# Attention of a two-layer encoder step: the query tiles of all heads as one stream, long and short in turn, decode last in each head, and later reads of y

## The chip, the cores and the metric

The program runs on one core of a Trainium2 chip. The metric is device time of one execution in microseconds (us); the number for a kernel is the median of its runs. Engines are named as in the profile: PE (TensorE; PEld is its weight load), DVE (VectorE), ACT (ScalarE), POOL (GpSimd) and SP (SyncE, which issues the DMAs).

## What is computed

Two layers, each over 1024 prompt tokens and 8 x 16 decode tokens (1152 rows, width 1024). All arithmetic is fp32; the large matrices are held as a high and a low part, so a product is three matmuls.

```
h = x @ w_in                      # pool_x, pool_gate, q, k, v, att_gate, merge_gate_a, merge_gate_b
A = (mean-pool mixer of pool_x) * silu(pool_gate)
s = q . k * 64**-0.5              # two maps (m = 0, 1) per head, 8 heads, rotary q and k
p = softmax(s);  a = p[0] - lam * p[1];  o = a @ v
B = rms_norm(o) * subln * (1 - lam_init) * silu(att_gate)
merged = sigmoid(ga) * (A @ w_a) + sigmoid(gb) * (B @ w_b)
x = layer_norm(ALPHA * x + merged @ w_o)
```

The prompt's mask lets a query see all keys up to the end of its own chunk of 64, so query tile i (128 rows, i from 0 to 7) meets 128 * (i + 1) keys: tile 7 is eight times as long as tile 0. A decode query (the item "d") sees 256 cached keys and its 16 new ones.

## The kernel before

A layer has four parts: the v columns (lines 524 to 566), q, k, the pooling and some gate columns by a product with seven multiplications (572 to 747), the rest of branch A (753 to 949), then attention with its filler (951 to 1450), and last w_b and w_o with the layer norm (1452 to 1615). The change lies in the attention part.

**Two generators are woven together there.** attention() (1280) does the heads; filler() (968) does the 16 remaining gate weights, in 384 units of three matmuls of 384 columns (line 320 to 322), with a tanh on ACT (977) after every eight units and, for the first eight weights, a product on DVE (980). attention() yields numbers; the loop at 1390 multiplies each by share (1388) and runs that many filler units, so that PE has work while softmax is under way. The numbers stand in the table STEPS (48): per item of a head a first number f1 and a second f2.

**One item of a head** goes through these pieces, each in program order on its engines:

- s1_tile (1054): scores on PE, for each m one product with the high and one with the low part of k, into ps_two, a pair of PSUM banks of which there are two. Tiles up to 3 take one pair, tiles 4 to 7 take both. soft() is its second half: DVE masks and takes the maximum (1072, or 1094 for the long ones), ACT does exp into p (1076, 1096), of which there are three buffers (one per short tile, two per long one).
- mix_tile (1101): DVE forms p[0] - c * p[1] (1105 to 1109).
- s2a_tile (1111): PE transposes the mixed p, ACT copies it out to at (1121).
- s2b_tile (1140): PE multiplies at with v, DVE copies the result (1126); do_squares then has ACT sum the squares (1130).
- "d" has the same pieces: s1_dec (1149), mix_dec, s2a_dec (1185; ten reductions on DVE, 1196 and 1198, between the transposes and the products), s2b_dec (1202).

An item's order before (1295 to 1356): s1(i); s2a of an earlier item; soft(i); squares; f1 filler; s2b of that earlier item; mix(i); f2 filler. The earlier item is two back up to n = 5, then one back; at n = 5 a second one is done, with a third number of filler. The items of a head run d, 0, 1, ... 7 (in the first head 0, 1, d, 2, 3, ... as line 1298 has it). After the last head, tile 7 is turned with a number 3 of filler and no other item beside it (1357 to 1359).

Loads for the next head are spread over the items: load_dec (1016, cached keys and new q, k, v), load_vc (1040, cached values), load_v (1010), prep_load and prep_split (881, 894: the two maps of q and k, split by two casts on ACT and two subtractions on DVE), mk_qz (1032).

**The read of y.** A head's result goes to memory (1247) and is read back (1260) when the gates of a token group are done, in the program's loop y_step (1368): it is issued, and two calls of y_step later ACT casts it into xh (1267), which waits for the transfer; DVE subtracts (1270). w_b multiplies it after that.

Of the kernel before, what the change touches and what calls it, by code (L numbers as in the profile page):

```python
# [11 lines left out]
F32 = mybir.dt.float32  # L12
# [5 lines left out]
P = 128  # L18
# [8 lines left out]
NG = 3  # L27
# [19 lines left out]
           11: (("x", 0, "t1"),), 12: (("s", 1),), 13: (("x", 1, "t2", "t3", "t4"),), 14: (("x", 1, "t1"),)}  # L47
STEPS = [(3, 2), (2, 2), (4, 1), (2, 2), (2, 2), (3, 3, 4), (3, 4), (3, 4), (4, 4)]
MG = 4
HIP = False  # L50
HEAD0 = 8
YG = 2
ENTRY_SLOTS = (1, 2, 4, 5)
# [10 lines left out]
def trunk(ctx, tc, a):  # L64
# [393 lines left out]
    for l in range(DEPTH):  # L458
# [494 lines left out]

        for tag, shape, bufs in (("osb", [P, 9, P], 2), ("gsb", [P, GW], 2), ("th", [P, GW], 3), ("atl", [P, P], 1),
                                 ("at", [P, 512], 2)):
            ap.tile(shape, F32, tag=tag, name=tag, bufs=bufs)
        for name in ("qs0", "kh0", "kl0"):
            ap.tile([P, SEQ], F32R, tag=name, name=name)
        ap.tile([P, 1024], F32, tag="p", name="p", bufs=3)
        cmask = ap.tile([P, 2, P], F32, name="cmask")  # L960
# [46 lines left out]
        groups_done = []  # L1007
        ITEMS = ["d", 0, 1, 2, 3, 4, 5, 6, 7]

# [126 lines left out]
        def do_squares():  # L1136
            while squares:
                squares.pop(0)()
# [141 lines left out]
        def attention():  # L1280
            def s2a(h, i):
                s2a_dec(h) if i == "d" else s2a_tile(h, i)
# [6 lines left out]

            load_dec(0)  # L1290
            load_v(0, 0)
            load_v(0, 1)
            prep_split(0, 1)
            yield HEAD0
            for h in range(H):
                start_head(h)
                nxt = h + 1 < H
                items = ITEMS if h else [0, 1, "d"] + ITEMS[3:]
                for n, i in enumerate(items):
                    f1, f2 = STEPS[n][:2]  # L1300
                    soft = s1_dec(h) if i == "d" else s1_tile(h, i)
                    if n == 0:
                        if h > 0:
                            s2a(h - 1, 7)
                    elif n >= 6:
                        s2a(h, items[n - 1])
                    elif n >= 2:
                        s2a(h, items[n - 2])
                    soft()
                    do_squares()  # L1310
                    yield f1
                    if n == 0:
                        if h > 0:
                            s2b(h - 1, 7)
                    elif n >= 6:
                        s2b(h, items[n - 1])
                    elif n >= 2:
                        s2b(h, items[n - 2])
                    mix(h, i)
                    if n == 5:  # L1320
                        s2a(h, items[4])
                        yield STEPS[n][2]
                        s2b(h, items[4])
                    if h == 0 and n == 0:
                        load_vc(0)
                    if h == 0 and n == 1:
                        mk_qz(0)
                    if h > 0:
                        if n == 1:
                            post_a(h - 1)  # L1330
                            g_load(h - 1, 0)
                            g_load(h - 1, 1)
                            load_v(h, 1)
                        if n == 2:
                            post_f(h - 1)
                        if 4 <= n <= 6:
                            post_b(h - 1, n - 4)
                        if n == 4:
                            g_load(h - 1, 2)
                        if n == 6:  # L1340
                            posted.append(h - 1)
                    if nxt:
                        if n == (2 if h else 3):
                            prep_load(h + 1, 0)
                        if n == 4:
                            load_dec(h + 1)
                        if n == 5:
                            prep_split(h + 1, 0)
                            prep_load(h + 1, 1)
                            load_v(h + 1, 0)  # L1350
                        if n == 7:
                            mk_qz(h + 1)
                        if n == 8:
                            prep_split(h + 1, 1)
                            load_vc(h + 1)
                    yield f2
            s2a(H - 1, 7)
            yield 3
            s2b(H - 1, 7)
            post_a(H - 1)  # L1360
# [7 lines left out]
        def y_step():  # L1368
# [7 lines left out]
            while ytodo and len(ylive) < 3:  # L1376
                (h, n), g = ytodo[0]
                if g not in groups_done or len(posted) < H - 1:
                    break
                ytodo.pop(0)  # L1380
                y_load(h, n, g)
                ylive.append([h, g, 2])

# [3 lines left out]
        W.use_f = False  # L1387
        share = len(gate_order) * NG * KD / (H * sum(map(sum, STEPS)) + HEAD0)
        due = 0.0
# [336 lines left out]
```

## Time and profile before

| what | before |
|---|---|
| median of 3 runs | 2411.27 us (2409.47 to 2414.34) |
| the profiled execution's own time | 2411.42 us |
| its span, first to last instruction | 2409.6 us |
| granted TensorE clock, mean | 0.993 |
| PE busy | 2304.1 us |
| PE weight loads busy | 2157.8 us |
| DVE busy | 1546.1 us |
| ACT busy | 977.8 us |
| attention of the first layer | from 558.7 us (first score) to about 1020 us |
| attention of the second layer | from 1752.8 us to about 2214 us |

The span lies 1.8 us under the execution's own time. In the profile L12 is line 12 of the kernel; a row of groups reads line, engine, operation, out<-in, shape, count, then busy time and the mean of one, then the engine's idle time before them and what ended it. A row of a table by stretches reads start:end, length, then for each engine its busy time with the number of its instructions, the granted clock of TensorE (1.00 is full), the DMA share and GB/s.

### The profile page before, as it was taken

To read this page: it belongs to the slowest core of one execution; us is meant where nothing else is said; L and a number is where in the kernel's file an instruction comes from. 1 tells how busy PE (TensorE), PEld (TensorE's weight loads), DVE (VectorE), ACT (ScalarE), POOL (GpSimd) and SP (SyncE) were. 2 spreads that over 40 slices of the span, in tenths; PEclk is the share of its full clock that TensorE was granted. 3 is DMA by queue.
4 is the path that set the end of the run, shared out by engine and by line. 5 is a ranking of instruction groups with operands and counts; after the bars stand their busy time and mean duration, and the time that the engine had idled before them with its cause. 6 is when DMAs were issued, how large, how long until landed. Compare 5 with 4: busy or idle time off the path is not lost.

```text
span 2409.6 us, 39819 instructions
## 1 busy us (share of the span) xinstructions
PE 2304.1 (96%) x14928; PEld 2157.8 (90%) x14928; DVE 1546.1 (64%) x2980; ACT 977.8 (41%) x2177; POOL 296.6 (12%) x312
## 2 busy tenths in 40 slices
PE   7999999998999999999999999999989999999998
PEld 6889999998888888898878999999988888889986
DVE  4477855546777777756524787546367777775855
ACT  8432234213555555523533232342145555554122
POOL 1023310000000000032100233000000000001433
PEclk9999999999999999999999999999999999999999
DMA  6643344656544554486336433445664555446942
GB/s 214 219 116 102 103 104 108 200 174 203 150 139 140 151 165 128 152 288 249 122 118 202 115 101 99 116 116 175 201 180 140 146 161 161 145 120 207 316 166 78
DMA packets 247714, 379.09 MB, mean 157 GB/s; under 512 B 49889, under 2 KB 190177, under 8 KB 247521
## 3 DMA queue, kind: packets, MB, share of 16 engines
q1 hardware_dynamic: 247520, 376.55, 50.9%
q8 instruction: 117, 1.92, 0.3%
q14 instruction: 77, 0.62, 0.1%
HBM read 259.67 MB, written 117.83 MB: 157 GB/s over the span
## 4 chain that ended last, share of the span: by engine, by line
PE 70%; DVE 11%; DMA 7%; ACT 6%; issue 4%; SPq 1%; POOL 1%; ACTq 0%; DVEq 0%; POOLq 0%
PE ps_lin L598 5%; PE ps_lin L596 5%; PE ps_lin L597 5%; PE ps_lin L320 5%; PE ps_lin L321 5%; PE ps_lin L322 5%; PE ps_tr L1144 4%; PE ps_tr L596 2%; PE ps_tr L598 2%; PE ps_tr L597 2%; PE ps_lin L335 2%; PE ps_lin L336 2%; PE ps_lin L334 2%; ACT p L1076 2%; PE ps_tr L1119 2%
## 5 line engine op out<-in xcount | busy, mean ns | idle before, releaser
L320 PE MATMUL ps_lin<-xh,wh 128*128 128x384 f32 x952 | 345.3, 363 | 1.1 <-ACT xh L1267 0.7
L322 PE MATMUL ps_lin<-xh,wl 128*128 128x384 f32 x952 | 321.3, 337 | 0.0
L321 PE MATMUL ps_lin<-xl,wh 128*128 128x384 f32 x952 | 320.7, 337 | 0.3 <-DVE xl L1270 0.2
L320 PEld LDWEIGHTS ps_lin<-xh,wh 128*128 128x128 f32 x952 | 180.4, 189 | 5.6 <-issue 2.8
L1144 PE MATMUL ps_tr<-vt,at 128*128 128x128 f32 x1152 | 156.2, 282 | 28.1 <-ACT at L1121 28.1
L1144 PEld LDWEIGHTS ps_tr<-vt,at 128*128 128x128 f32 x1152 | 147.2, 195 | 39.2 <-ACT at L1121 38.6
L321 PEld LDWEIGHTS ps_lin<-xl,wh 128*128 128x128 f32 x952 | 180.8, 190 | 1.1 <-DVE xl L1270 0.8
L322 PEld LDWEIGHTS ps_lin<-xh,wl 128*128 128x128 f32 x952 | 179.5, 189 | 0.0
L1121 ACT COPY at<-ps_tr 128x512 f32<-128x512 f32 (+1 forms) x192 | 85.8, 482 | 172.1 <-PE ps_tr L1119 172.1
L1096 ACT ACTIVATE p<-ps_two,anm 128x640 f32<-128x640 f32 (+3 forms) x128 | 122.3, 962 | 33.4 <-DVE anm L1094 29.8
L1076 ACT ACTIVATE p<-ps_two,anm 128x128 f32<-128x128 f32 (+3 forms) x128 | 66.4, 524 | 168.6 <-DVE anm L1072 160.3
L1094 DVE TENSOR_REDUCE anm<-ps_two 128x1 f32<-128x640 f32 (+3 forms) x128 | 131.2, 1025 | 4.4
L270 DVE TENSOR_TENSOR wl<-ws,wh 128x1024 fp32r<-128x1024 f32 (+1 forms) x74 | 86.0, 1162 | 70.8 <-ACT wh L265 67.6
L265 ACT CAST wh<-ws 128x1024 fp32r<-128x1024 f32 (+1 forms) x74 | 74.1, 1002 | 115.4 <-PE ps_lin L321 49.7
L640 POOL TENSOR_TENSOR tt<-tt 128x288 f32<-128x288 f32 x64 | 63.1, 986 | 420.4 <-DVE tt L639 257.2
L1108 DVE SCALAR_TENSOR_TENSOR p<-p,acc 128x128 f32<-128x128 f32 (+7 forms) x128 | 104.8, 818 | 4.5
L1086 PE MATMUL ps_two<-kh,qs 128*128 128x320 f32 (+3 forms) x256 | 91.0, 357 | 11.3 <-ACT p L1076 11.3
L1119 PE MATMUL ps_tr<-ident,p 128*128 128x128 f32 x576 | 84.4, 273 | 5.6 <-DVE r L1109 5.6
L1087 PE MATMUL ps_two<-kl,qs 128*128 128x320 f32 (+3 forms) x256 | 89.5, 352 | 0.0
L1126 DVE COPY osb<-ps_tr 128x128 f32<-128x128 f32 x144 | 41.3, 287 | 66.1 <-PE ps_tr L1144 60.4
L659 ACT COPY sb<-ps_lin 128x288 f32<-128x288 f32 x80 | 32.0, 400 | 123.3 <-PE ps_lin L598 118.8
L1119 PEld LDWEIGHTS ps_tr<-ident,p 128*128 128x128 f32 x576 | 69.2, 141 | 13.0 <-ACT xh L1267 6.2
(522 smaller groups left out, 6886.9 us busy)
## 6 DMA issues: line engine op xcount, KB each, us to landing
ws<-wt SPq DMA_DIRECT2D x96, 512.0 KB, 4.0
mt_d<-th SPq DMA_DIRECT2D x96, 192.0 KB, 3.2
fx<-q_d SPq DMA_DIRECT2D x128, 128.0 KB, 3.4
fx<-o_k SPq DMA_DIRECT2D x128, 128.0 KB, 3.3
st<-ck SPq DMA_DIRECT2D x32, 512.0 KB, 5.9
fx<-cv SPq DMA_DIRECT2D x32, 512.0 KB, 4.0
mt<-mt_d SPq DMA_DIRECT2D x42, 384.0 KB, 5.8
xT_d<-xs SPq DMA_DIRECT2D x36, 256.0 KB, 2.6
```

Source lines behind the costliest of these rows:

```text
L320: PE.matmul(ps, wh[:, k, :], xh[:, k, :], start=(k == 0), stop=False),
L321: PE.matmul(ps, wh[:, k, :], xl[:, k, :], start=False, stop=False),
L322: PE.matmul(ps, wl[:, k, :], xh[:, k, :], start=False, stop=(k == nk - 1)))
L596: PE.matmul(ps, wh[:, k, :], oh[:, k, :], start=first and k == 0, stop=False, **more)
L597: PE.matmul(ps, wh[:, k, :], ol[:, k, :], start=False, stop=False, **more)
L598: PE.matmul(ps, wl[:, k, :], oh[:, k, :], start=False, stop=k == 3, **more)
L1076: S.activation(out=pt[m], in_=s[:, m, :n], func=AF.Exp, bias=nm[:, m:m + 1], accum_out=ls_[:, m:m + 1])
L1094: V.tensor_reduce(out=nm[:, m:m + 1], in_=s[:, :, :c], axis=AX.XY, op=ALU.max, negate=True)
L1096: S.activation(out=p[:, :n].rearrange("p (b c) -> p b c", b=2), in_=s[:, :, :c], func=AF.Exp, bias=nm[:, m:m + 1], accum_out=ls_[:, m:m + 1])
L1108: V.scalar_tensor_tensor(out=pt[0], in0=pt[1], scalar=cc, in1=pt[0], op0=ALU.mult, op1=ALU.add)
L1119: PE.transpose(tr[:, j * P:(j + 1) * P], p[:, (b0 + j) * P:(b0 + j + 1) * P], ident)
L1144: PE.matmul(o_ps, hd["at", i][b // 4][:, (b % 4) * P:(b % 4 + 1) * P], hd["vt", b // 4][:, b % 4, :], start=(b == 0), stop=(b == i))
```

## The change

The heads become one list, flow, of (head, position n, item) triples, with the items of a head in the order 7, 3, 6, 2, 5, 1, 4, 0, d (in the last head 7, 3, 6, 2, 5, d, 4, 1, 0). At each step j the program does s1 of item j, s2a of item j - 2, soft of item j, mix of item j - 1, squares, f1 filler, s2b of item j - 2, f2 filler. So every item is turned two steps after its scores, across the border of heads too, and its mix is one step later than before and stands behind the next item's maximum on DVE. The doubled step n = 5 and its third number go.

share leaves REST = 28 units of the filler out of attention; what is left runs after it. STEPS sums to 52 per head instead of 54.

The loads move: load_dec and load_vc are of the same head now (n = 2 and n = 8; in the last head load_vc at n = 3), mk_qz at n = 6 (last head: 4), load_v's second half at n = 0, prep_split of map 1 before the scores of n = 8; post_a, post_f and post_b at n = 2, 3 and 5 to 7.

A read of y is cast five calls of y_step after its issue instead of two. Last, the list that reserved tiles at the head of the attention pool goes, so its tiles lie at other addresses.

```
-STEPS = [(3, 2), (2, 2), (4, 1), (2, 2), (2, 2), (3, 3, 4), (3, 4), (3, 4), (4, 4)]
+STEPS = [(2, 3), (5, 1), (3, 2), (3, 4), (3, 2), (3, 4), (3, 2), (3, 3), (3, 3)]
+REST = 28
...
-        ITEMS = ["d", 0, 1, 2, 3, 4, 5, 6, 7]
+        ITEMS = [7, 3, 6, 2, 5, 1, 4, 0, "d"]
+        LAST = [7, 3, 6, 2, 5, "d", 4, 1, 0]
...
+            flow = [(h, n, i) for h in range(H) for n, i in enumerate(ITEMS if h < H - 1 else LAST)]
+            for j in range(len(flow) + 2):
+                h, n, i = flow[j] if j < len(flow) else (H, j - len(flow), None)
+                back = flow[j - 2] if j >= 2 else None
...
+                if n == 8 and not last:
+                    if h + 1 < H:
+                        prep_split(h + 1, 1)
+                soft = None
+                if i is not None:
                     soft = s1_dec(h) if i == "d" else s1_tile(h, i)
...
+                if back:
+                    s2a(back[0], back[2])
+                if soft:
                     soft()
+                if 0 < j <= len(flow):
+                    mix(flow[j - 1][0], flow[j - 1][2])
+                do_squares()
+                yield f1
+                if back:
+                    s2b(back[0], back[2])
...
-                ylive.append([h, g, 2])
+                ylive.append([h, g, 5])
...
-        share = len(gate_order) * NG * KD / (H * sum(map(sum, STEPS)) + HEAD0)
+        share = (len(gate_order) * NG * KD - REST) / (H * sum(map(sum, STEPS)) + HEAD0)
```

Each engine has as many instructions of each kind as before; only their places differ. Three places follow.

**ACT, fourth head of the first layer.** Before, the stretch in the middle of the head, from the copy of tile 2's transposes (at, 384 columns) to the casts for the next head. L1096 is exp, L1130 a square, L977 the filler's tanh, L265 the split of a filler weight, L902 and L903 the casts of the next head's q and k.

```order
L1121 COPY at<-ps_tr 128x384
L1096 ACTIVATE p,als<-ps_two,anm 128x640 x2
L1130 ACTIVATE jk,ss<-osb 128x128
L977 ACTIVATE th<-ps_lin 128x384
L265 CAST wh<-ws 128x1024
L1121 COPY at<-ps_tr 128x512
L902 CAST qs<-fx 128x1024
L903 CAST kh<-fx 128x1024
```

After, the same head from tile 7's copies on: L1117 is the copy, L1092 and L1072 exp, L972 the tanh.

```order
L1117 COPY at<-ps_tr 128x512 x2
L1092 ACTIVATE p,als<-ps_two,anm 128x896 x2
L1126 ACTIVATE jk,ss<-osb 128x128 x2
L1117 COPY at<-ps_tr 128x512
L1072 ACTIVATE p,als<-ps_two,anm 128x384 x2
L972 ACTIVATE th<-ps_lin 128x384
L1117 COPY at<-ps_tr 128x512
L1117 COPY at<-ps_tr 128x384
L1092 ACTIVATE p,als<-ps_two,anm 128x768 x2
```

Before, the copy of tile 3 (512 columns) stands behind tile 4's exp of the same step, a square, a tanh and a cast. After, each step's copies stand ahead of that step's exp and behind the exp of the step before.

**DVE, the decode item at the start of the fifth head of the first layer.** Before: mix of tile 0 (L1108), the previous head's post_a (L1224 to L1226), the ten reductions of the decode item (L1196, L1198), then the maximum of tile 1.

```order
L1108 SCALAR_TENSOR_TENSOR p<-p,acc 128x128
L1109 RECIPROCAL r_8287<-als 128x1
L1224 TENSOR_TENSOR wv__8383<-r_7629 128x9
L1225 TENSOR_TENSOR wv__8383<-wv__8383,ss 128x9
L1226 TENSOR_SCALAR wv__8383<-wv__8383 128x9
L1196 TENSOR_REDUCE azt<-ps_tr 128x2x16 x4
L1198 TENSOR_REDUCE atl<-ps_tr 128x64
L1196 TENSOR_REDUCE azt<-ps_tr 128x2x16 x4
L1198 TENSOR_REDUCE atl<-ps_tr 128x64
L1071 MEMSET ps_two 64x2x64
L1072 TENSOR_REDUCE anm<-ps_two 128x2
```

After: the same ten reductions (L1192, L1194, of the fourth head's decode item) stand at n = 1 of the fifth head.

```order
L1192 TENSOR_REDUCE azt<-ps_tr 128x2x16 x4
L1194 TENSOR_REDUCE atl<-ps_tr 128x64
L1192 TENSOR_REDUCE azt<-ps_tr 128x2x16 x4
L1194 TENSOR_REDUCE atl<-ps_tr 128x64
L1067 MEMSET ps_two 64x2x64
L1068 TENSOR_REDUCE anm<-ps_two 128x2
L1101 RECIPROCAL ar_8259<-als 128x1
L1103 SCALAR_TENSOR_TENSOR acc<-als,nlam,ar_8259 128x1
L1104 SCALAR_TENSOR_TENSOR p<-p,acc 128x1024
L1105 RECIPROCAL r_8174<-als 128x1
L1122 COPY osb<-ps_tr 128x128
```

They stand ahead of tile 3's maximum (L1068) and of tile 7's mix (L1104, 1024 columns), which the next step's transposes read.

**ACT, end of the first layer's attention.** Before, with the casts of y (L1267) and the last two tiles:

```order
L1267 CAST xh<-fx 128x2x384
L1121 COPY at<-ps_tr 128x512
L1121 COPY at<-ps_tr 128x384
L1096 ACTIVATE p,als<-ps_two,anm 128x1024 x2
L1130 ACTIVATE jk,ss<-osb 128x128
L1267 CAST xh<-fx 128x384
L1267 CAST xh<-fx 128x2x384 x3
L1121 COPY at<-ps_tr 128x512 x2
L977 ACTIVATE th<-ps_lin 128x384
```

After, with L1263 for the casts of y, and tile 0 as the last:

```order
L1072 ACTIVATE p,als<-ps_two,anm 128x128 x2
L1126 ACTIVATE jk,ss<-osb 128x128
L972 ACTIVATE th<-ps_lin 128x384
L1117 COPY at<-ps_tr 128x256
L1126 ACTIVATE jk,ss<-osb 128x128
L972 ACTIVATE th<-ps_lin 128x384
L1263 CAST xh<-fx 128x2x384 x2
L1117 COPY at<-ps_tr 128x128
L1126 ACTIVATE jk,ss<-osb 128x128
L1263 CAST xh<-fx 128x2x384
```

Before, four casts of y stand between tile 7's exp and the copies of tile 7, the last of the attention; after, two stand between tile 0's exp and its one copy.

More of the change, by code (lines that the diff above doesn't have):

```diff
@@ L952, in trunk @@
         ap = ap_ctx.enter_context(tc.tile_pool(name=f"a2_{l}", bufs=1, reuse_waits="tile"))
[L954 to L959, printed above, removed]
         cmask = ap.tile([P, 2, P], F32, name="cmask")
@@ L1288, in mix @@
                 mix_dec(h) if i == "d" else mix_tile(h, i)
-            load_dec(0)
             load_v(0, 0)
@@ L1294, in attention @@
             yield HEAD0
[L1295 to L1300, printed above, removed]
-                    soft = s1_dec(h) if i == "d" else s1_tile(h, i)
[L1302 to L1308, printed above, removed]
-                    soft()
[L1310 to L1319, printed above, removed]
-                    if n == 5:
[L1321 to L1343, printed above, removed]
-                            prep_load(h + 1, 0)
[L1345 to L1356, printed above, removed]
@@ L1357, in attention @@
-            s2a(H - 1, 7)
-            yield 3
-            s2b(H - 1, 7)
+            flow = [(h, n, i) for h in range(H) for n, i in enumerate(ITEMS if h < H - 1 else LAST)]
+            for j in range(len(flow) + 2):
+                h, n, i = flow[j] if j < len(flow) else (H, j - len(flow), None)
+                back = flow[j - 2] if j >= 2 else None
+                last = h == H - 1
+                f1, f2 = STEPS[n]
+                if n == 0 and h < H:
+                    start_head(h)
+                if n == 8 and not last:
[3 more added lines that the diff above has]
+                if i is not None:
+                    soft = s1_dec(h) if i == "d" else s1_tile(h, i)
+                if back:
+                    s2a(back[0], back[2])
+                if soft:
+                    soft()
+                if 0 < j <= len(flow):
[4 more added lines that the diff above has]
+                    s2b(back[0], back[2])
+                if h > 0 and n == 0 and h < H:
+                    load_v(h, 1)
+                if 0 < h < H:
+                    if n == 2:
+                        post_a(h - 1)
+                        g_load(h - 1, 0)
+                        g_load(h - 1, 1)
+                    if n == 3:
+                        post_f(h - 1)
+                    if 5 <= n <= 7:
+                        post_b(h - 1, n - 5)
+                    if n == 5:
+                        g_load(h - 1, 2)
+                    if n == 7:
+                        posted.append(h - 1)
+                if h < H:
+                    if n == 2:
+                        load_dec(h)
+                        if h + 1 < H:
+                            prep_load(h + 1, 0)
+                    if n == 3 and last:
+                        load_vc(h)
+                    if n == (4 if last else 6):
+                        mk_qz(h)
+                if h + 1 < H:
+                    if n == 5:
+                        prep_split(h + 1, 0)
+                        prep_load(h + 1, 1)
+                        load_v(h + 1, 0)
+                    if n == 8:
+                        load_vc(h)
+                yield f2
```

## The prediction

> **What bounds the kernel now.** I read the page first, then a table by stretches (one stretch per head of the attention), then PE's waits inside the attention, then the timeline of one wait.
>
> ```profile
> PE 2304.1 (96%) x14928; PEld 2157.8 (90%) x14928; DVE 1546.1 (64%) x2980; ACT 977.8 (41%) x2177; POOL 296.6 (12%) x312
> ```
>
> PE is the bound: 2304.1 of 2409.6 us busy, so 105.5 us idle in all. The change has as many instructions of each kind as before, hence PE's own work stays and only its idle time and its clock can move. The heads of the first layer, with PE, PEld, DVE, ACT and POOL busy in each stretch and then the clock:
>
> ```profile
> 558.00:604.00 46.00, 40.00 (x275) 36.41 (x274) 32.07 (x80) 19.98 (x56) 0.00 (x0) 0.96 0.67 196
> ...
> 660.00:715.00 55.00, 51.21 (x371) 47.46 (x370) 42.11 (x102) 28.70 (x77) 2.11 (x3) 1.00 0.48 142
> ...
> 934.00:989.00 55.00, 53.90 (x392) 50.30 (x391) 38.13 (x98) 29.10 (x81) 2.00 (x2) 1.00 0.28 89
> 989.00:1020.00 31.00, 27.30 (x155) 25.65 (x153) 20.52 (x35) 17.09 (x32) 2.00 (x2) 0.89 0.57 177
> sum 462.00, PE 431.45 PEld 400.64 DVE 339.31 ACT 244.45 POOL 16.62; mean PE 47.94 PEld 44.52 DVE 37.70 ACT 27.16 POOL 1.85
> ```
>
> And the second layer's attention in the same cut:
>
> ```profile
> 1752.00:1798.00 46.00, 38.83 (x267) 35.14 (x266) 30.59 (x78) 18.78 (x53) 0.00 (x0) 0.96 0.65 195
> ...
> 2183.00:2214.00 31.00, 27.33 (x162) 25.27 (x160) 21.84 (x36) 17.34 (x32) 2.00 (x2) 0.94 0.59 181
> sum 462.00, PE 430.46 PEld 399.17 DVE 339.47 ACT 244.34 POOL 16.62; mean PE 47.83 PEld 44.35 DVE 37.72 ACT 27.15 POOL 1.85
> ```
>
> PE is idle 462 - 431.45 = 30.6 us in one layer's attention and 462 - 430.46 = 31.5 us in the other: 62.1 of the 105.5 us. It is worst at the start (6.0 us of 46), about 3.8 us in the third head (55 - 51.21), 1.1 us near the end of the heads, and 3.7 us again after them. Its clock falls below full in the first and the last stretch. What ended PE's waits in the first layer's attention:
>
> ```profile
> PE ps_tr L1144 <- ACT at L1121: 14.3, 14, 1.9
> PE ps_two L1086 <- ACT p L1076: 5.7, 7, 1.0
> ...
> PE ps_two L1157 <- DMA vt<-o_v: 2.6, 1, 2.6
> ```
>
> Twenty of the 30.6 us are ACT's: the copy of transposes before the product with v, and exp, which frees the scores' PSUM; a load ends just one wait, of 2.6 us. One wait for a copy on ACT's timeline, in the fourth head:
>
> ```profile
> 755.71 0.80 ACT L1096 ACTIVATE p<-ps_two,anm 128x640 f32<-128x640 f32 x1
> ...
> 756.78 0.48 ACT L977 ACTIVATE th<-ps_lin 128x384 f32<-128x384 f32 x1
> 757.16 1.04 ACT L265 CAST wh<-ws 128x1024 fp32r<-128x1024 f32 x1
> 758.09 0.59 ACT L1121 COPY at<-ps_tr 128x512 f32<-128x512 f32 x1
> ```
>
> The copy is the last of a queue: exp, tanh and cast go first, and PE's product with v comes only after it. ACT is busy for 28.7 of the 55 us of the head before, so this is its order and not its load.
>
> **The change part by part.** *The stream.* With the copies ahead of their step's exp, a copy waits only for what ACT has left over from the step before. Such a step lasts about 5.5 us: a head's busy PE time is 51.2 us and loses 3.4 of its 47.1 filler units (54 x 0.873 before, 52 x 0.840 after). A unit by PE's timeline:
>
> ```profile
> 992.24 0.35 PE L320 MATMUL ps_lin<-xh,wh 128*128 128x384 f32 x1
> ...
> 992.78 0.33 PE L320 MATMUL ps_lin<-xh,wh 128*128 128x384 f32 x1
> ```
>
> One unit is 0.54 us from start to start, so a head has 51.2 - 3.4 x 0.54 = 49.4 us of PE work in nine steps. ACT has 28.7 us per head, 3.2 per step, and between transposes and product stand some 2.5 units, 1.35 us, against a copy of 0.59. I take both ACT waits as gone in most steps. Long and short items in turn also mean that tiles 4 to 7, which take both PSUM pairs, never follow one another.
>
> *What is late next is DVE.* It has 42.1 us per head; in heads of 49.4 us that is 85%, where it was 77%. Its durations in the fourth head:
>
> ```profile
> L980 DVE SCALAR_TENSOR_TENSOR th<-th,ps_lin 128x384 f32<-128x384 f32 x5 | 2.8, 550 | 3.6 <-ACT th L977 3.6
> L1108 DVE SCALAR_TENSOR_TENSOR p<-p,acc 128x1024 f32<-128x1024 f32 x2 | 2.6, 1284 | 0.1
> L1126 DVE COPY osb<-ps_tr 128x128 f32<-128x128 f32 x9 | 2.6, 284 | 1.9 <-PE ps_tr L1144 1.4 <-PE ps_tr L1214 0.5
> ...
> L1094 DVE TENSOR_REDUCE anm<-ps_two 128x1 f32<-128x1024 f32 x2 | 2.4, 1224 | 0.1
> L270 DVE TENSOR_TENSOR wl<-ws,wh 128x1024 fp32r<-128x1024 f32 x2 | 2.4, 1214 | 0.0
> ...
> L1072 DVE TENSOR_REDUCE anm<-ps_two 128x2 f32<-128x1024 f32 x1 | 1.2, 1224 | 0.0
> L1196 DVE TENSOR_REDUCE azt<-ps_tr 128x32 f32<-128x64 f32 x8 | 1.2, 216 | 0.0
> ...
> L1198 DVE TENSOR_REDUCE atl<-ps_tr 128x64 f32<-128x128 f32 x2 | 0.6, 282 | 0.0
> ```
>
> The narrowest place is n = 1, where the decode item's ten reductions stand ahead of tile 3's maximum and tile 7's mix. From tile 7's scores to its mix DVE has two maxima (2.45), a copy (0.28), ten reductions (8 x 0.216 + 2 x 0.282 = 2.29), tile 3's maximum (1.22) and the mix (1.28): 7.5 us, and 9.5 us with the masks, reciprocals and the decode item's scaling, which I put at 2. If a filler weight falls there, L980 and L270 add 1.76: 11.3 us. PE takes two steps, 11 us, to the transposes that read the mix. So it fits, or is late by up to 1 us when a weight falls there; L270 also waits for ACT's cast. Ends: nothing per head, or today's 3.8 us. I take 1.2 us, nearer the sum than today's row, which is another queue's.
>
> *The ends.* The first score now starts with tile 7 instead of tile 0, and the decode item of the first head, third before, comes ninth. The last item is tile 0 instead of 7. The rows, with PE busy and then the clock:
>
> ```profile
> 558.90:561.40 2.50, 1.00 (x6) 1.00 0.79 224
> 565.80:568.70 2.90, 0.41 (x3) 1.00 0.90 211
> 570.00:574.50 4.50, 4.50 (x24) 0.62 0.53 190
> 996.00:999.40 3.40, 0.62 (x4) 1.00 0.77 211
> 1001.00:1002.50 1.50, 0.82 (x4) 0.50 0.49 127
> ```
>
> The 1.5 us at 558.9 (the split of the second map is late) stays by 0.8, since the four longer products of the first map cover the rest. The 2.5 us before the decode item (its values were still loading) and the 2.8 us before tile 7's transposes go. In the last head the decode reductions, 2.29 us, have three yields, 2.5 units or 1.35 us, of cover: 0.9 us is lost there, new. The later cast of y means that ACT no longer waits for a transfer ahead of an exp or a copy; y's chain then has the filler that runs after the attention as cover (28 units less 9 in the stream's two last steps, 19 x 0.54 = 10.3 us), without which it would cost up to the 3.7 us of today's last stretch. I keep 0.5 us for it. The loads that move on SP (load_dec beside prep_load at n = 2, load_vc) are issued five or more us ahead of their use, and no wait of the heads after the first is for a load today: nothing, or at worst one wait of 2.5 us per layer like that of the first head. The reserved tiles change addresses and first waits only: nothing, within the same bound.
>
> *The clock.* The row at 0.62 follows the 2.5 us wait, the one at 0.50 the 2.8 us wait. Over the stretches the loss is 46 x 0.04 + 31 x 0.11 in the first layer and 46 x 0.04 + 31 x 0.06 in the second: 9.0 us. It goes with those waits. The Trainium skill, page "TensorE: Matmul & The Clock Gate", section "What's actually happening", has half rate come after an idle window of about 3.4 us. Here 2.5 us were enough, so the measurement decides.
>
> *The sum.* Lost now: 62.1 idle and 9.0 clock, 71.1 us. Kept: per layer 8 x 1.2 + 0.8 + 0.9 + 0.5 = 11.8, for two 23.6 us. Gain 47.5 us. The profiled execution took 2411.4 us, 0.1 us from the median; 2411.4 - 47.5 = 2364 us.
>
> **The rivals.** *DVE takes over in part.* Each of the first five heads of a layer, where L980 runs, keeps 3.8 us: 5 x 3.8 + 3 x 1.2 + 2.2 = 24.8 per layer, gain 71.1 - 49.6 = 21.5, time 2390 us. For it: 85% of a strictly ordered queue, with each mix behind the next item's maximum, which itself waits for PE. Against: today the five slower heads have the decode item's wait as well, and DVE idles 13 us per head.
>
> *It slows down: one long wait per head at n = 1 or n = 2.* If reductions, cast, split, maximum and mix line up so that the transposes of tile 7 come late by 2.8 us in every head, the clock halves each time, which cost 4.5 x 0.38 = 1.7 us after the first decode wait. That is 4.5 us, plus 1.2 elsewhere, in 16 heads: 91 us, plus 4.4 at the ends, against 71.1 saved: 2436 us. It decides from a wait of about 2.5 us on; shorter ones only eat the gain. For it: DVE's sum of 9.5 to 11.3 us against 11. Against: it must be late in all heads, and the second half of a layer has no L980. By the Trainium skill's 3.4 us (the same page and section) a 2.8 us wait would leave the clock alone, and the time would be 2409 us; the rows of this case speak for the halving.
>
> *No change in effect.* The waits move and cost what they did, within 4.8 us. Little speaks for it: ACT's order is changed for certain, and a DVE that had just this much too little time would be chance.
>
> *More than forecast.* 0.3 us kept per head: 2 x (2.4 + 2.2) = 9.2, time 2350 us; and each wait that goes also saves a short restart of PE that its idle time doesn't show, so down to 2342.
>
> **How the numbers follow.** Forecast with its better end (2342 to 2380) 64%, DVE in part (2380 to 2402) 24%, no change 4%, slower 8%. The range from 2342 to 2396 leaves out the slower case, no change, and the ends. A measurement tells about 0.2% (4.8 us) from no change: faster 0.88, same 0.04, slower 0.08.
>
> **What would show it.** Right: PE's waits for at and p nearly absent from the attention, PE idle there below 15 us per layer, DVE at 80% or more of it, full clock in the first and last stretch, the waits left on DVE's mix or the decode reductions. Wrong: a wait of PE of over 2 us that repeats in every head, a clock below 0.95 in stretches in the middle, or ACT waiting for y's transfer ahead of a copy.

## The result

The changed kernel takes 2348.6 us (median of four runs, 2347.1 to 2351.2) against 2410.8 us for the kernel before in the same session. The ratio is 0.974, 95% interval 0.972 to 0.976: faster by 62 us, where 47.5 were forecast. Its profiled execution took 2349.3 us with a span of 2347.5 us, against 2409.6 us, so the spans differ by 62.1 us and the two traces can be laid side by side.

### The profile page after: what moved, and what is told of

Its sections match the earlier page's. It is cut to its first block, busy times and chain, and to the rows that moved or that the text cites. A ratio compares the mean times of both kernels' runs of the same rounds, so it can differ in the third digit from the quotient of the medians.

```text
span 2347.5 us, 39899 instructions
## 1 busy us (share of the span) xinstructions
PE 2288.2 (97%) x14928; PEld 2150.2 (92%) x14928; DVE 1538.9 (66%) x2980; ACT 981.8 (42%) x2177; POOL 301.8 (13%) x312
## 4 chain that ended last, share of the span: by engine, by line
PE 82%; DVE 6%; DMA 5%; ACT 3%; issue 3%; SPq 1%; POOL 1%; DVEq 0%; ACTq 0%; POOLq 0%
PE ps_lin L321 7%; PE ps_lin L322 6%; PE ps_lin L323 6%; PE ps_tr L1140 5%; PE ps_lin L597 5%; PE ps_lin L599 5%; PE ps_lin L598 5%; PE ps_tr L1115 3%; PE ps_tr L597 3%; PE ps_tr L599 2%; PE ps_tr L598 2%; PE ps_lin L336 2%; PE ps_lin L337 2%; PE ps_lin L335 2%; PE ps_two L1082 2%
## 5 line engine op out<-in xcount | busy, mean ns | idle before, releaser
L1117 ACT COPY at<-ps_tr 128x512 f32<-128x512 f32 (+2 forms) x192 | 86.8, 482 | 191.8 <-PE ps_tr L1115 191.6
L1140 PE MATMUL ps_tr<-vt,at 128*128 128x128 f32 x1152 | 150.0, 275 | 0.0
L1090 DVE TENSOR_REDUCE anm<-ps_two 128x1 f32<-128x1024 f32 (+3 forms) x128 | 131.1, 1024 | 4.4
L1092 ACT ACTIVATE p<-ps_two,anm 128x1024 f32<-128x1024 f32 (+3 forms) x128 | 122.3, 963 | 25.4 <-DVE anm L1090 22.3
L1104 DVE SCALAR_TENSOR_TENSOR p<-p,acc 128x1024 f32<-128x1024 f32 (+7 forms) x128 | 104.8, 819 | 4.5
L1072 ACT ACTIVATE p<-ps_two,anm 128x512 f32<-128x512 f32 (+3 forms) x128 | 66.5, 524 | 79.5 <-DVE ar L1101 59.9
L1115 PE MATMUL ps_tr<-ident,p 128*128 128x128 f32 x576 | 85.6, 273 | 6.4 <-ACT at L1117 4.1
L1082 PE MATMUL ps_two<-kh,qs 128*128 128x512 f32 (+3 forms) x256 | 90.0, 355 | 1.5 <-ACT p L1072 1.2
L1083 PE MATMUL ps_two<-kl,qs 128*128 128x512 f32 (+3 forms) x256 | 89.1, 351 | 0.7 <-DVE kl L906 0.7
L1115 PEld LDWEIGHTS ps_tr<-ident,p 128*128 128x128 f32 x576 | 68.7, 141 | 12.1 <-ACT at L1117 5.5
L1508 POOL TENSOR_TENSOR mg<-mt 128x384 f32<-128x384 f32 x42 | 60.0, 1433 | 115.2 <-DVE mt L1507 115.2
```

The lines of the kernel that those rows point to most:

```text
L1082: PE.matmul(s[:, b, :c], qs[:, ql], kh[:, kc], start=True, stop=False)
L1090: V.tensor_reduce(out=nm[:, m:m + 1], in_=s[:, :, :c], axis=AX.XY, op=ALU.max, negate=True)
L1092: S.activation(out=p[:, :n].rearrange("p (b c) -> p b c", b=2), in_=s[:, :, :c], func=AF.Exp, bias=nm[:, m:m + 1], accum_out=ls_[:, m:m + 1])
L1104: V.scalar_tensor_tensor(out=pt[0], in0=pt[1], scalar=cc, in1=pt[0], op0=ALU.mult, op1=ALU.add)
L1115: PE.transpose(tr[:, j * P:(j + 1) * P], p[:, (b0 + j) * P:(b0 + j + 1) * P], ident)
L1140: PE.matmul(o_ps, hd["at", i][b // 4][:, (b % 4) * P:(b % 4 + 1) * P], hd["vt", b // 4][:, b % 4, :], start=(b == 0), stop=(b == i))
```

## The profile after

The first part of the page, the engines' busy time in the changed kernel:

```profile
PE 2288.2 (97%) x14928; PEld 2150.2 (92%) x14928; DVE 1538.9 (66%) x2980; ACT 981.8 (42%) x2177; POOL 301.8 (13%) x312
```

PE has the same 14928 instructions and is busy 15.9 us less; its idle time falls from 105.5 to 59.3 us. To see where, the run is cut at the same events in both kernels: from the first score of a layer's attention to the last transposes of its results, and from there to the end of the product that follows. In each row the columns are the stretch and its length, PE, PEld, DVE, ACT and POOL busy, the clock, the DMA share and GB/s. The kernel before:

```profile
558.90:1018.20 459.30, 428.95 (x3045) 398.53 (x3045) 337.53 (x802) 243.18 (x634) 16.62 (x22) 0.99 0.50 150
1018.20:1108.20 90.00, 89.65 (x517) 89.07 (x516) 57.07 (x65) 24.60 (x30) 29.02 (x22) 1.00 0.86 298
1753.00:2211.40 458.40, 427.46 (x3045) 396.96 (x3044) 336.77 (x801) 242.74 (x634) 16.62 (x22) 0.99 0.50 150
2211.40:2301.80 90.40, 89.80 (x517) 89.01 (x516) 63.74 (x69) 12.58 (x14) 34.03 (x23) 1.00 0.89 313
```

The changed kernel, in the same four stretches:

```profile
560.20:984.80 424.60, 418.78 (x3047) 393.55 (x3045) 331.98 (x799) 243.43 (x632) 20.29 (x25) 1.00 0.54 161
984.80:1078.50 93.70, 91.17 (x516) 88.91 (x514) 58.62 (x68) 26.12 (x33) 29.26 (x22) 1.00 0.86 290
1720.60:2146.10 425.50, 418.83 (x3045) 393.37 (x3044) 333.27 (x799) 243.66 (x632) 20.29 (x25) 1.00 0.54 161
2146.10:2239.70 93.60, 92.22 (x517) 90.60 (x516) 64.20 (x71) 13.99 (x16) 33.37 (x23) 0.98 0.86 305
```

The two attentions together are 67.6 us shorter. Of that 48.8 us are idle time of PE (30.35 + 30.94 before, 5.82 + 6.67 now), and 18.8 us are busy time of PE for the same number of matmuls. The stretch behind each attention is longer by 3.7 and 3.2 us, 6.9 us given back. All the other stages make 1.4 us.

PE's waits in the first layer of the changed kernel, from just ahead of the first score on; the second layer's are the same but for the start, where PE waits 0.26 and 0.69 us for the split of the first head's maps:

```profile
PE ps_tr L1115 <- ACT at L1117: 2.0, 3, 0.7
PE ps_tr L1188 <- DVE osb L1122: 1.5, 2, 0.7
PE ps_tr L1115 <- DVE osb L1122: 1.2, 2, 0.7
PE ps_lin L321 <- DVE th L941: 1.1, 1, 1.1
PE ps_two L1082 <- ACT p L1072: 0.6, 1, 0.6
```

The 14 waits of PE's product for ACT's copy are gone; the three waits for a copy that are left are waits of transposes (L1115). In place of the seven waits for exp there are one of 0.6 us and another of 0.2. No wait in the attention is for the mix (L1104), for the decode reductions or for a load. The wait of 1.1 us lies just ahead of the first score; the longest behind it is 0.7 us, and the clock is 1.00 in both attentions.

## The experiments

The theory to start from was the prediction's: the copies stand ahead of their step's exp, the alternation keeps tiles 4 to 7 from following one another, the filler held back covers y's chain, and DVE at n = 1 is what comes next. A part that does nothing is the rival in each case. Every run was timed beside the kernel before, which took 2411.3 to 2412.0 us in these sessions.

**The distance between a read of y and its cast.**

```diff
-                ylive.append([h, g, 5])
+                ylive.append([h, g, 2])
```

> The changed kernel with y's cast two passes behind its read, as before the change, instead of five. Theory (the later reads and casts of y give part of the gain back): behind the attention the last cast of a read comes at 982.79 us and holds the direct casts of the last head back, so that PE waits 1.5 us there and runs nine products in 4.9 us instead of 1.6, 3.3 us per layer. With two passes the last read and its cast come several us earlier, these waits go and the time falls to about 2342 us. Rival (the twelve reads take 29 us whatever the distance, 951.4 to 980.3 in the changed kernel and 982.7 to 1011.4 in the one before): nothing is won behind the attention, and ACT waits for the transfer ahead of a copy again, which cost PE one wait of 3.1 us in a layer of the kernel before: 2349 to 2355 us.

> The changed kernel with y's cast three passes behind its read instead of five. Theory (late casts cost 3.3 us per layer behind the attention): between the result for two passes and 2348.6 us, nearest to two, about 2343 us. Rival (the pace of the reads is set elsewhere): 2348 to 2351 us.

Measured: 2349.8 us with two passes and 2347.7 with three, ratios 0.974 (0.973 to 0.976) and 0.973 (0.972 to 0.975). Neither differs from the changed kernel, so the rival holds: the later reads of y are worth nothing by themselves. The reads' first and last start, in the changed kernel and then with two passes:

```profile
L1256 SPq DMA_DIRECT2D fx<-y_d x12: 319/370/440, 951.4 to 980.3; - x12
```

```profile
L1256 SPq DMA_DIRECT2D fx<-y_d x12: 319/379/460, 950.6 to 978.9; - x12
```

Twelve reads take 28.9 and 28.3 us. The code says why: a group of y may be read only when the filler has done with that group's columns, and the third group's filler is the last of all. In the changed kernel its four reads start at 973.1 us and later, and PE leaves the filler at 972.4.

**No filler held back.**

```diff
-REST = 28
+REST = 0
```

> The changed kernel with no filler held back for the time behind the attention (28 units of 0.54 us are shared out among the steps as before). My prediction's term says that this filler covers y's chain: without it PE waits behind the attention by up to 15 us less what the chain now leaves, and the more filler in the heads can only win the 5 to 6 us per layer that PE still waits there; by it the time is 2358 us or more, up to 2375. Rival (y's passes are counted in filler units, so the chain shrinks with the filler, and the stream gains cover): 2345 to 2350 us.

Measured: 2365.3 us, 16.7 us more, so the prediction's term holds in sign, and its size lies near the middle of the expected range. PE's waits of this run in the last stretch of the first layer (955 to 995 us):

```profile
PE ps_tr L1140 <- ACT at L1117: 3.4, 2, 1.8
PE ps_two L322 <- DVE xl L1266: 1.7, 3, 1.0
```

The last tiles' copies come late, and the products wait for y's casts. So the 3.4 us for the copies are not those of y's chain behind the attention: on ACT one of the two copies stands behind the cast of a weight (1.04 us) and the other behind three casts of y (2.30 us).

**The same filler held back in the kernel before.**

```diff
-        share = len(gate_order) * NG * KD / (H * sum(map(sum, STEPS)) + HEAD0)
+        share = (len(gate_order) * NG * KD - 28) / (H * sum(map(sum, STEPS)) + HEAD0)
```

> The kernel before with one thing changed: 28 units of filler are held back for the time behind its attention, as in the changed kernel. Theory (the filler held back covers y's chain, and the run without it cost the changed kernel 8.3 us per layer): the last stretch of the attention, which loses 3.7 us to waits and about as much to the clock, gets most of that back, and the heads, which lose half a unit per step, give some of it up: 2398 to 2408 us. Rival (the heads of the kernel before need their filler as cover for the waits for copies and exps): 2411 to 2430 us.

Measured: 2421.1 us, ratio 1.0039 (1.0026 to 1.0052), slower by 9.4. The rival holds. So the 28 units are a gain only in the new stream. The stretch behind the attention shows something else in this run:

```profile
1021.10:1114.20 93.10, 91.89 (x517) 90.42 (x516) 58.25 (x66) 25.13 (x31) 28.85 (x21) 0.98 0.85 289
2219.10:2312.30 93.20, 91.98 (x516) 90.30 (x515) 62.66 (x71) 13.04 (x15) 32.44 (x23) 0.98 0.88 306
```

It is 3 us longer than in the kernel before, as it is in the changed kernel, and PE waits there for the same casts (0.46 and 0.45 us in each layer). With the filler held back, the 3 us lost there appear in the old order too.

**The reserved tiles.** The list that the change removed is put back.

```diff
+        for tag, shape, bufs in (("osb", [P, 9, P], 2), ("gsb", [P, GW], 2), ("th", [P, GW], 3), ("atl", [P, P], 1),
+                                 ("at", [P, 512], 2)):
+            ap.tile(shape, F32, tag=tag, name=tag, bufs=bufs)
...
         cmask = ap.tile([P, 2, P], F32, name="cmask")
```

> The changed kernel with the list of reserved tiles of the kernel before put back (osb, gsb, th, atl, at, the first head's maps and p are allocated ahead of the masks). Theory (it moves addresses and first waits only, which I put at nothing): 2348.6 us within 2. Rival (the reserved order makes the first head wait for buffers of the stage before, a wait of 2.5 us per layer as the bound had it): 2351 to 2354 us.

Measured: 2351.1 us, ratio 0.975 (0.973 to 0.976) against 0.974 (0.972 to 0.976): no difference that can be told. The median lies at the edge of the rival's range, but PE's waits in the first attention are those of the changed kernel, with none of 2.5 us. They cost nothing that these runs can tell, as forecast.

**One step behind instead of two.**

```diff
-                back = flow[j - 2] if j >= 2 else None
+                back = flow[j - 1] if j >= 1 else None
...
-                if 0 < j <= len(flow):
-                    mix(flow[j - 1][0], flow[j - 1][2])
                 do_squares()
                 yield f1
                 if back:
                     s2b(back[0], back[2])
+                if i is not None:
+                    mix(h, i)
```

> The changed kernel with every tile turned one step behind its scores instead of two; the mix then stands in the tile's own step, behind the product of the tile before. Order of the items, fillers and y stay. Theory (the second step is what takes the chain from the scores to the turning off PE's path): for a long tile two maxima (2.45 us), the second exp (0.8), and the mix (1.28) make 4.5 us ahead of the transposes, a step lasts 5.5 us of which the scores themselves take about 1, so PE waits 0.5 to 1.5 us in each of the 64 long steps, 32 to 96 us, and the time is 2380 to 2440 us. Rival (the alternation and the filler at the end carry the gain): 2348 to 2355 us.

Measured: 2501.6 us, 153 us more than the changed kernel and 90 more than the one before. The theory holds in sign, and its size was too small: the time lies 62 us beyond the range. PE's waits in the first layer:

```profile
PE ps_tr L1115 <- DVE r L1105: 25.1, 16, 2.3
PE ps_tr L1115 <- DVE p L1104: 16.4, 8, 2.9
```

Twenty-four transposes wait for the mix, or for the small operation that stands right behind it. The edit changes two things, since the mix then stands ahead of the next maxima again. The run that follows has that order of mix and maxima with the lag of two; against its 2418.1 us the second step of lag alone is worth 83 us.

**The mix ahead of the next maxima, and then ascending tiles.** The lag of two steps and the copies ahead of the exps stay in both.

```diff
+                if 0 < j <= len(flow):
+                    mix(flow[j - 1][0], flow[j - 1][2])
                 if soft:
                     soft()
-                if 0 < j <= len(flow):
-                    mix(flow[j - 1][0], flow[j - 1][2])
```

> The changed kernel with the mix of the tile before put ahead of the maxima of the next tile instead of behind them (the transposes' copies stay ahead of the exps). It is the control for the run with the tiles in ascending order, which needs this for its buffers. Theory (DVE has room, since PE's waits left in the changed kernel are 0.4 us per head and none is for the mix): 2346 to 2353 us. Rival (DVE is near its limit, and the maxima that come 1.28 us later hold the PSUM pairs and so the next scores): at least 0.5 us in each of 64 long steps, 2380 us or more.

Measured: 2418.1 us, ratio 1.003 (1.002 to 1.004). The theory was wrong and the rival holds: this one swap on DVE undoes the whole gain. PE's waits in the first layer of this run:

```profile
PE ps_two L1082 <- ACT p L1072: 12.5, 9, 2.3
PE ps_two L1063 <- ACT p L1092: 9.1, 8, 2.4
```

The waits are for exp, which has to free the PSUM pair that the next scores need. DVE in the fourth head, where tile 7's mix (L1104) now goes ahead of tile 3's maximum (L1068):

```profile
731.15 1.28 DVE L1104 SCALAR_TENSOR_TENSOR p<-p,acc 128x1024 f32<-128x1024 f32 x1
...
732.72 1.22 DVE L1068 TENSOR_REDUCE anm<-ps_two 128x2 f32<-128x1024 f32 x1
```

and ACT, idle for 4.73 us until that maximum is there, and PE's scores of tile 6 behind it:

```profile
734.04 0.69 ACT L1072 ACTIVATE p<-ps_two,anm 128x512 f32<-128x512 f32 x1 [4.73 <-DVE anm L1068]
```

```profile
735.54 0.47 PE L1082 MATMUL ps_two<-kh,qs 128*128 128x448 f32 x1 [1.13 <-ACT p L1072]
```

The mix is needed only a step later, the maximum at once. The kernel before had this order as well, since each mix stood in its own tile's step. On its DVE, ahead of the copy that the prediction showed, tile 4's maximum stands behind tile 3's mix and a product of the head before (L1243, 0.60 us), though the scores of tile 4's first map had been there since 751.1:

```profile
752.38 0.75 DVE L1108 SCALAR_TENSOR_TENSOR p<-p,acc 128x512 f32<-128x512 f32 x1
...
753.87 0.82 DVE L1094 TENSOR_REDUCE anm<-ps_two 128x1 f32<-128x640 f32 x1
```

ACT's exp of tile 4, which heads the queue in front of that copy, waits for this maximum:

```profile
754.73 0.80 ACT L1096 ACTIVATE p<-ps_two,anm 128x640 f32<-128x640 f32 x1 [1.08 <-DVE anm L1094]
```

Then, with the mix first, the tiles in ascending order:

```diff
-        ITEMS = [7, 3, 6, 2, 5, 1, 4, 0, "d"]
-        LAST = [7, 3, 6, 2, 5, "d", 4, 1, 0]
+        ITEMS = [0, 1, 2, 3, 4, 5, 6, 7, "d"]
+        LAST = [0, 1, 2, 3, 4, "d", 5, 6, 7]
```

> The changed kernel with the mix first, and the tiles of a head in ascending order, 0 to 7 and then the decode item (in the last head the decode item sixth), so that the long tiles 4 to 7 follow one another; the lag of two steps, fillers and y stay. Theory (long and short in turn matter because tiles 4 to 7 take both PSUM pairs): the waits for exp of the kernel before come back, 5.7 us per layer there, so 11 us more than the run with the mix first alone, some more with DVE's load bunched in four steps: about 2360 to 2375 us. Rival (the lag of two steps is all that counts): within 3 us of the run with the mix first.

Measured: 2434.5 us, 16.4 more than with the mix first alone, against 11 and some more expected. Its largest wait in the first layer:

```profile
PE ps_two L1082 <- ACT p L1092: 18.0, 11, 3.3
```

Long scores wait for the exp of the long tile before them. With the mix first, the alternation is worth 16 us. With the mix behind the maxima the ascending order wasn't tried, because two long tiles in a row then need four buffers for p, and the kernel has three.

**The alternation alone, in the kernel before.**

```diff
-        ITEMS = ["d", 0, 1, 2, 3, 4, 5, 6, 7]
+        ITEMS = ["d", 0, 4, 1, 5, 2, 6, 3, 7]
...
-                items = ITEMS if h else [0, 1, "d"] + ITEMS[3:]
+                items = ITEMS if h else [0, 4, "d", 1] + ITEMS[4:]
```

> The kernel before with one thing changed: the items of a head in the order d, 0, 4, 1, 5, 2, 6, 3, 7 (in the first head of a layer 0, 4, d, 1, 5, 2, 6, 3, 7); its lags (two steps, and one from the seventh item on), fillers and y stay. Theory (order alone isn't the gain, the lag of one step behind the last items stays): the waits for the copy stay at about 14 us per layer and those for exp go, 2395 to 2410 us. Rival (the order of the tiles is most of the gain): 2360 to 2375 us.

Measured: 2443.9 us, slower than the kernel before by 32.5, outside what either side expected, and the waits went the other way than the theory had it: those for the copy fall from 14.3 to 2.7 us in the first layer, and those for exp grow to

```profile
PE ps_two L1086 <- ACT p L1076: 20.8, 10, 3.4
```

from 5.7 us. The transposes (L1119) also wait 11.6 us for DVE there (2.8 us in the kernel before). So the order of the tiles alone, with the mix ahead of the maxima and a lag that changes in the middle of a head, is a loss; which of the two makes it one was not tried.

**How much room DVE has at n = 1.** Tile 3's maximum is taken once and twice more.

```diff
                     V.tensor_reduce(out=nm, in_=s[:, :, :n], axis=AX.X, op=ALU.max, negate=True)
+                    if i == 3:
+                        for _ in range(1):
+                            V.tensor_reduce(out=nm, in_=s[:, :, :n], axis=AX.X, op=ALU.max, negate=True)
```

> The changed kernel with the maximum of tile 3 taken twice (1.22 us more on DVE in each head, at the place where my sum put 9.5 to 11.3 us of DVE's work against 11 us of time). Theory (the mix of tile 7 is in time with little to spare: by the trace it ends 0.9 to 1.6 us ahead of PE's first transpose that reads it, least in the first, third and fifth head): late by 0.3 us in three or four heads per layer, 2349 to 2352 us. Rival (DVE has room, its order was the only trouble): 2348.6 us, and so still with the maximum taken three times. Second rival (DVE is late already, as my sum had it): 1.2 us in each of 16 heads, 2368 us.

> The changed kernel with the maximum of tile 3 taken three times (2.45 us more on DVE in each head). Theory (0.9 to 1.6 us to spare ahead of the transposes of tile 7): 2.45 less the spare time of each head makes 10.0 us per layer, 20 us in all, some more with the clock where a wait comes to 2.5 us: 2365 to 2375 us. Rival (DVE has room): within 3 us of 2348.6. Second rival (DVE is late already): 2.45 us in 16 heads, 2388 us or more.

Measured: 2368.8 and 2398.4 us, 20 and 50 more. Both lie beyond my theory's ranges and where "late already" had them (2368 us, and 2388 or more); the room ahead of the transposes, on which my theory rested, isn't what counts. Both runs' waits for exp in the first layer's attention (L1085 and L1075 here are L1082 and L1072 of the changed kernel):

```profile
PE ps_two L1085 <- ACT p L1075: 6.6, 8, 1.8
```

```profile
PE ps_two L1085 <- ACT p L1075: 16.7, 8, 3.1
```

One wait in every head, and in the third head it is this one:

```profile
670.77 0.47 PE L1085 MATMUL ps_two<-kh,qs 128*128 128x448 f32 x1 [1.10 <-ACT p L1075]
```

Tile 6's second map waits for tile 3's exp. The same place in the changed kernel, DVE's maximum and mix first:

```profile
665.38 1.22 DVE L1068 TENSOR_REDUCE anm<-ps_two 128x2 f32<-128x1024 f32 x1
...
666.96 1.28 DVE L1104 SCALAR_TENSOR_TENSOR p<-p,acc 128x1024 f32<-128x1024 f32 x1
```

and then ACT and PE:

```profile
667.37 0.68 ACT L1072 ACTIVATE p<-ps_two,anm 128x512 f32<-128x512 f32 x1
...
668.20 0.47 PE L1082 MATMUL ps_two<-kh,qs 128*128 128x448 f32 x1
```

The exp ends at 668.05, and the score starts 0.15 us behind it. In the runs with more DVE work every such wait ends 0.14 us behind the exp, so that is the least that these runs show, and the third head has nothing to spare. By the same reading the eight heads of a layer have 0 to 0.9 us to spare, and the first of them waits for 0.61 us in the changed kernel. Adding 1.22 us to these eight gives the eight waits of the run to within 0.15 us each. That the first run meets the 2368 us of "late already" is luck: that side had 1.2 us of wait in every head, while the waits added are 6.0 us per layer, 12.0 in all, and the rest of the 20 us is mostly PE's busy time in the two attentions (843.0 us against 837.6).

**The last head's casts ahead of y's last ones.**

```diff
         part_step(0)
+        post_b(H - 1, 0, direct=True)
+        g_load(H - 1, 2)
         part_step(1)
+        post_b(H - 1, 1, direct=True)
...
-        for g in range(NG - 1):
-            post_b(H - 1, g, direct=True)
-            if g == 0:
-                g_load(H - 1, 2)
```

> The changed kernel with the last head's own results for the first two groups turned, split and cast between the first two parts of the product with w_o, ahead of the last casts of y's reads, instead of behind them. Theory (the four reads of the third group can start only when the filler is at its end, at 973.1 us in the changed kernel, so that their last cast comes 11 us later, and the three casts of the last head queue behind it, 1.67 us each): two of the three leave that queue, and of the 3.3 us per layer 1.7 to 3.3 are won, 2342 to 2345 us. Rival (the last read alone sets the end): 2347 to 2350 us; and if the casts of the last head hold ACT or DVE up ahead of the filler's last tanh or the casts of weights, up to 2353 us.

Measured: 2352.3 us, ratio 0.9755 (0.9742 to 0.9768): nothing won, as in the second rival. ACT of this run near the end of the first attention:

```profile
976.04 0.51 ACT L1263 CAST xh<-ysb 128x384 fp32r<-128x384 f32 x1 [1.26 <-DVE ysb L1239]
980.04 0.51 ACT L1263 CAST xh<-ysb 128x384 fp32r<-128x384 f32 x1 [3.48 <-DVE ysb L1239]
980.45 2.29 ACT L1263 CAST xh<-fx 128x768 fp32r<-128x768 f32 x3
```

ACT waits 3.48 us for the last head's second group, and the three casts of y's reads stand behind it; PE then waits 2.0 us for one of them, earlier than before. The queue was only turned round.

## Why the prediction was right, and where it was not

The sign and the range were right, and so was the bound: the time was in PE's idle time and clock inside the attention. The sum came out 14.6 us short. Its terms, and what the two traces measure:

| term, both layers | forecast, us | measured, us |
|---|---|---|
| idle time of PE in the attention | -38.5 | -48.8 |
| clock and busy time of PE there | -9.0 | -18.8 |
| behind the attention | 0 | +6.9 |
| other stages | 0 | -1.4 |
| sum | -47.5 | -62.1 |

*The stream.* "With the copies ahead of their step's exp, a copy waits only for what ACT has left over" is right as far as it goes. The 14 waits of the product for the copy are gone, and they stay away in the run with the mix first (two, 0.8 us in all), which has the same lag and the same order of copies and exps. But that run loses the whole gain, to waits for exp: 21.6 us in the first layer by the two rows shown, against 5.7 in the kernel before. These exps wait for DVE, for maxima that stand behind a mix. So the place of the mix behind the next maxima is what the gain hangs on, and the prediction named it only in a rival, as a reason why DVE would be late. In the row at 755.71 I saw a full queue on ACT, read it as ACT's order, and didn't look at what had made the exp late, the 1.08 us at 754.73. The second step of lag is needed as well (83 us without it), because only with it can the mix stand behind the next maxima.

*DVE at n = 1.* The place was right and the waiter wrong. I asked whether tile 7's mix reaches the transposes in time. It does in all 16 heads, by 0.9 to 1.6 us, so the 1.2 us per head that I kept is zero: the term was too large by about 19 us. The chain that is tight there is tile 3's maximum, its exp, and tile 6's scores, with 0 to 0.9 us to spare, and it costs 0.6 us per layer. Waits that my sum did not have took part of the place: 4.7 us per layer for DVE's copies of results and for the copy of transposes.

*The ends.* The split of the first head's maps was put at 0.8 us; it costs 0.95 in the second layer (0.26 and 0.69) and, within the stretch, nothing in the first. The last head's decode item was put at 0.9 us; between its transposes (945.92) and its products (948.26) PE has no wait, so this term is zero. (The wait of 0.73 us at 911.16 in the last head is for the copy of a result, ahead of the transposes of the seventh head's decode item.) For y's chain I kept 0.5 us per layer, counted in the table's first row. This is the term that failed: the chain holds the end back behind the attention. In the second layer of the changed kernel the nine products that close the first three parts take 4.7 us there instead of 1.6, and in the first layer 4.4. Two of their rows, the first of the second and of the third three:

```profile
2148.05 0.44 PE L321 MATMUL ps_two<-xh,wh 128*128 128x384 f32 x1 [0.46 <-ACT xh L1263]
...
2149.71 0.44 PE L321 MATMUL ps_lin<-xh,wh 128*128 128x384 f32 x1 [0.45 <-ACT xh L1263]
```

Three products take 1.66 us, where 0.52 us is their pace without waits. In the second layer the clock then falls to half for some 3 us, which the stretch's 0.98 shows; in the first layer two waits of 0.60 and 0.56 us for a later product on DVE (L1507) come on top, which are not y's. The cover of 10.3 us of filler that I named ends just where the third group's reads may begin, so it cannot cover them. That the reads go by the filler's groups stood in the code, and I had not followed it.

*The clock.* Its term was right: 1.00 in both attentions. PE's busy time fell by as much again, since a matmul behind a wait takes longer. Worked out from the two traces, the half clock adds 8.0 us to the two attentions before and nothing after, and the matmuls right behind a wait add 16.8 us to their usual pace before (63 waits) and 5.7 after (23 waits). I had named these restarts, but only for the better end of the range.

*Loads and reserved tiles* cost nothing, as put. DVE is busy 78% of the first attention (331.98 of 424.6 us), just under the 80% named.

*The rivals.* "DVE takes over in part" (2390 us) and "one long wait per head" (2436 us) did not come, but they were near: 2.45 us more on DVE per head gave 2398 us. "More than forecast" (2350 us) has the measured time, but by luck: it kept 9.2 us of idle time where 12.5 are left in the attentions, and had nothing for the 6.9 us behind them; some 10 us of restarts, which it named only for its lower end, make up for both.

What stays open is how the 3 us behind each attention could be won. They come with the filler held back, also in the kernel before; neither an earlier cast nor another order of the casts won them. The new counts of filler per step, the place of the decode item and the moved loads were not tried by themselves.

## What to carry to other kernels

On an in-order engine that serves two chains, put the work that frees a resource ahead of the work that is needed a step later: to put the maxima, on which the exp that frees PSUM waits, ahead of the mix was worth 69.5 us here, and it needed the second step of lag to be possible at all. When a wait names a late copy, follow the queue one engine further before calling it that engine's order. Parts of such a change aren't added up one by one: the alternation (with the mix first) and the filler held back are gains in the new stream, and each was a loss by itself in the old one.

## What the runs showed of the chip

Waiting costs PE more than its idle time. With the same 3045 to 3047 matmuls in the first attention, PE is busy 418.8 us beside 5.8 us of idle time, 429.0 us beside 30.4 (before), and in the run with one step of lag:

```profile
558.60:1056.80 498.20, 440.47 (x3046) 403.73 (x3045) 335.16 (x799) 243.06 (x633) 18.12 (x25) 0.98 0.46 137
```

That is 440.5 us beside 57.7, or some 0.4 us more of busy time for each us of idle time, the clock's share included. (In that run's second layer, where the clock is 0.96, it is 0.56 us.)

No single length of wait decides when the clock falls. The run with two more maxima has the same waits in both layers, to within 0.02 us. The third head's, first layer and then second:

```profile
677.13 0.47 PE L1085 MATMUL ps_two<-kh,qs 128*128 128x448 f32 x1 [2.36 <-ACT p L1075]
```

```profile
1859.57 0.47 PE L1085 MATMUL ps_two<-kh,qs 128*128 128x448 f32 x1 [2.36 <-ACT p L1075]
```

PE's clock behind the third and fifth head's waits of 2.36 and 2.50 us, first layer and then second:

```profile
677.10:679.10 2.00, 1.97 (x13) 1.65 (x13) 1.96 (x6) 0.68 (x3) 0.00 (x0) 1.00 0.00 0
...
782.90:785.00 2.10, 2.10 (x14) 1.99 (x15) 2.02 (x7) 0.78 (x4) 0.00 (x0) 1.00 0.86 183
...
1859.60:1861.60 2.00, 2.00 (x10) 1.83 (x11) 1.96 (x6) 0.36 (x3) 0.00 (x0) 0.75 0.00 0
1861.60:1863.60 2.00, 2.00 (x9) 2.00 (x8) 1.93 (x4) 1.73 (x3) 0.00 (x0) 0.50 0.81 248
1966.90:1969.00 2.10, 2.10 (x7) 1.82 (x8) 1.58 (x6) 0.19 (x2) 0.00 (x0) 0.50 0.64 184
```

In the first layer the clock stays full, in the second it halves. Nor is a wait of that length needed. Behind the attentions of the changed kernel PE has the same waits in both layers, none over 0.46 us, and is busy for 2.57 of 3.80 us in the first and 2.53 in the second; the 3.4 us behind these, first layer and then second:

```profile
988.80:992.20 3.40, 3.26 (x19) 3.26 (x20) 3.01 (x6) 1.50 (x2) 1.10 (x2) 1.00 0.76 259
```

```profile
2150.20:2153.60 3.40, 3.29 (x10) 3.30 (x11) 2.56 (x5) 1.45 (x2) 1.14 (x2) 0.53 0.83 249
```

So the 2.5 us from which the prediction let the clock fall is no threshold. The Trainium skill, page "TensorE: Matmul & The Clock Gate", section "What's actually happening", has the idle time counted in a window that runs on by itself, which fits that equal waits end differently; its length of about 3.4 us is more than these waits, and there the measurement decides.
